# First modulation loads on two queues, with a new opening order: a two-layer decoder trunk on one Trainium2 core

## The chip, the cores and the metric

The kernel runs on one core of a Trainium2 chip. The metric is the device time of one execution in microseconds (us). Before the change the median of 3 runs is 1925.78 us (1925.18 to 1926.59). A core has a matrix engine (TensorE, PE in the profile; PEld is its weight load), a vector engine (VectorE, DVE), a scalar engine (ScalarE, ACT), GpSimd (POOL) and a sync engine (SP). Each works through its own list of instructions in order. A transfer is issued by one of them, here by SP or ACT, and is then moved by 16 DMA engines that all issuers share. Engines wait for each other, and for transfers, by semaphores.

## The reference

Two layers, 512 rows, 2048 columns, all in float32. Only the start matters here: the modulation of the first layer, and the first products of its input projection.

```python
c_act = jax.nn.silu(c)                                  # c: (1, 2048)
mod = c_act @ w_mod[l] + b_mod[l]                       # w_mod[l]: (2048, 6144)
shift, scale, gate = jnp.split(mod, 3, axis=-1)
h = x * (1.0 + scale[:, None]) + shift[:, None]         # x: (1, 512, 2048)
proj = h @ w_in                                         # w_in: (2048, 8192)
q, k, v, g = jnp.split(proj, 4, axis=-1)
```

Differential attention, an output projection and a layer norm follow, then a second layer with forgetting attention. The change touches none of that.

## The kernel before

**Products.** A float32 product is made of three fast ones: each operand is split into a rounded high part and the rest. `A` is high by high, `B` takes the rest of the input `h`, `C` the rest of the weights. A product is one matmul of 128x128 by 128x512.

**The opening** computes shift and scale of the first layer, builds `h` from them, and meanwhile runs the input projection of the first two heads (u = 0 and 1). The contraction of 2048 goes in 16 blocks of 128, `kt` = 0 to 15. Block `kt` of `h` needs columns `kt` of shift and of scale, and each of these columns is a sum over all 16 row blocks of `w_mod`. `SETS` orders these column blocks: first block 0 alone, then block 1 alone, then pairs. So the first set is 2 MB of `w_mod` (8 loads of 256 KB: two halves of 8 row blocks, each in two parts, each for shift and for scale), the second set another 2 MB, and every later set 4 MB.

The steps are single letters; each engine's order is a string of them (`ORDER_SP`, `ORDER_ACT`, `ORDER_PE`, `ORDER_DVE`, lines 41 to 44), written by a planner outside the kernel:

- SP: `L` is one load of `w_mod` into a tile `sms`, `X` a piece of `x` into `xt`, `W` a tile of projection weights `wst` (two transfers). W0 is the first tile for head 0's q and k (384 columns), W1 for its v and g, W2 and W3 the same for head 1.
- DVE: `d` adds one row block, times the matching value of `silu(c)`, to the running sum `sacc` (line 618; the first one of a set is line 616); `m` writes the finished columns of shift and scale to `mcol` (line 671); `b` makes the rest `wlo` of a weight tile (line 132), `l` the rest `hl` of a block of `h` (line 709).
- PE: `e` takes single row blocks of `w_mod` off DVE's hands (`PE_ROWS`: row blocks 6, 9, 10 and 13 of the first set, 9, 13 and 15 of the second); `o` sums `sacc` over its partitions; `t` transposes a block of `x`; `F` is a filler matmul with no result; `A`, `B`, `C` are the products (line 720).
- ACT: `a` casts a weight tile to its high part `whi` (line 125); `h` and `i` apply shift and scale to a transposed block of `x` (lines 694 and 701: `hh`, and `htmp` for the rest); `c` and `r` move partial sums out of PSUM and back.

So the first column goes: 12 `d` on DVE, `o` on PE, `m` on DVE, `h` on ACT, first product on PE. The same chain follows for block 1 and for each later set.

**Before the strings** a fixed prologue stands outside the opening's block: loads of `c` (`crow`) and of the biases (`brow`), their transposes, `silu(c)` into `cact`, the biases into `bcol`. All loads of the opening go through SP; eight loads of `w_mod` stand at the head of its string. A function `op_L` issues a load; it already takes a queue as an argument.

**Completion semaphores.** The framework hands eight completion semaphores (DMAHW0 to DMAHW7) to the transfers in turn. Each finished transfer adds 16. A transfer that takes a semaphore over waits, on the engine that issues it, until the transfer that had it before has landed.

Of the kernel before, what the change touches and what calls it, by code (L numbers as in the profile page):

```python
# [13 lines left out]
AF = mybir.ActivationFunctionType  # L14
ALU = mybir.AluOpType

P = 128
D = 2048
KT = D // P
# [18 lines left out]
PE_ROWS = {0: (6, 9, 10, 13), 1: (9, 13, 15)}  # L38
EARLY = (0,)
NBUF = 5  # L40
ORDER_SP = '8LX2LWLW7LX2LW2LW2LXW2LW4LWLWLXLWLWLW7LWLW3LWLX2L2WLW2LW3L2WLW2L2W2LW4LW2LWX4LW2L8Wp'
ORDER_ACT = 'ahiahia5ca2cahiahicracrcracrcrcrcrahiahia2c2rcrcrcrcracrahihi3ahiahicra2c2racrcrcracrhihai3ahihiacracrcrcrcracrcrhiahi3acracrcrcr3crc2r6c'
ORDER_PE = '4eFto7F3A3B3CABeCAB2eCABCABoCt7A7B7CABCABCABCABCABCABCABAB2CABCABCABCAoBCtABCABC2AtA3B3C6A6B5CACBCABCABCABCABCABCABCABCABCABCABCABCABCAoBCtABCABCABtCABCABCABCABCABCABCABCABCABCABCABCABCABCABCABCABCABCABCABCABoCABCABCABtCABCABCABtCABCABCABCABCABCABCABCABCABCABCABCABCABCABCABCAoBCtABCABC2AtA3B3C5A5B5CABCABCABCABCABCABCABCABCABCABCABCABCABCABCABCoABtCABCABCABtCABCABCABCABCABCABCABCABCABCABCABCABCABCABCABCABCABCABCABCABCABCABCAoBCABtCABCABCABtCABCABCABCABCABCABCABCABCABCABCABCABCABCABCABCABCABCABoCABtCABCABCABCABtCABCABCABCABCABCABCABCABCABCABCABCABCABCABCABCABCAB2AB2CBCABCABCABCABCABCABCABCABCABCABCABCABCABCABCABCABCABCABCABCABCABCABCABCABCABCABCABCABCABCABC'
ORDER_DVE = '13dm3dbldb9dm3dl3db5db4dmb2dldbl6db3db4dmb2dldbldb14dbmdb3dldl4db5dbmbdldbl6db3db5dbm5dbl3dbl6db2dbm4dl2dlb5db5dbmlbl4b'
MANUAL = {ET.DVE, ET.PE, ET.Activation, ET.SP}
CUT = False
LAM_INIT = 0.8 - 0.6 * math.exp(-0.0)
# [97 lines left out]
def tile_yoco(  # L145
# [23 lines left out]
    nc = tc.nc  # L169
    V, S, PE, G = nc.vector, nc.scalar, nc.tensor, nc.gpsimd  # L170
# [25 lines left out]
    def tr_bank(name="tr"):  # L196
        return ps.tile([P, 512], F32, name=name, tag="tr", bufs=1)
# [14 lines left out]
    def corner(sc, q, k):  # L212
# [6 lines left out]
    ident = const.tile([P, P], F32, name="ident")  # L219
# [3 lines left out]
    mask = const.tile([P, 512], F32, name="mask")  # L223
# [7 lines left out]
    crow, brow = (  # L231
        kpool.tile([P, T], F32, name=name, tag="K")[:k, 0:P]
        for name, k in (("crow", KT), ("brow", 32))
    )
    nc.sync.dma_start(crow, c[0].rearrange("(a p) -> a p", p=P))
    nc.sync.dma_start(brow, b_mod[0, 0 : 2 * D].rearrange("(a p) -> a p", p=P))
    ccol = const.tile([P, KT], F32, name="ccol")
    pcol = const.tile([P, 38], F32, name="pcol")
    bcol = const.tile([P, 2, KT], F32, name="bcol")
    pt = tr_bank()  # L240
    PE.transpose(pt[:, 0:KT], crow, ident[0:KT, 0:KT])
    V.tensor_copy(ccol, pt[:, 0:KT])
    cact = const.tile([P, KT], F32, name="cact")
    tc.keep_in_program_order(S.activation(cact, ccol, AF.Exp, scale=-1.0))
    V.tensor_scalar(cact, cact, 1.0, None, op0=ALU.add)
    V.reciprocal(cact, cact)
    V.tensor_tensor(cact, cact, ccol, op=ALU.mult)
    pt = tr_bank()
    PE.transpose(pt[:, 0:32], brow, ident[0:32, 0:32])
    V.tensor_copy(bcol[:, 0, :], pt[:, 0:16])  # L250
    V.tensor_scalar(bcol[:, 1, :], pt[:, 16:32], 1.0, None, op0=ALU.add)
    gcol, bncol = pcol[:, 0:16], pcol[:, 16:32]

    neglam = const.tile([P, 1], F32, name="neglam")
# [232 lines left out]
    with tc.tile_pool(name="start", bufs=2, reuse_waits="tile") as sp, tc.manual_schedule(engines=MANUAL):  # L487
        mcol = const.tile([P, 2, KT], F32, name="mcol")

        fill = kpool.tile([P, T], F32R, name="fill", tag="K")  # L490
        S.copy(fill[:, 0:384], mask[:, 0:384])
        tiles = []
        for i, (k0, nk) in enumerate(sets):
            nr = 8 // nk
# [41 lines left out]
        cnt = dict.fromkeys("LXWpdmlbahicretoABCF", 0)  # L536
# [22 lines left out]
        def op_L(j, queue=None):  # L559
            n, kq, step, v = loads[j]  # L560
            i, k, nr = tiles[n]
            k0, nk = sets[i]
            if n not in mtile:
                if n >= NBUF and not rows_read(n - NBUF):
                    return False
                mtile[n] = sp.tile([P, nr, 2, nk * P], F32, name="sms", tag="sms", bufs=NBUF)
            rows = w_mod[0, (k + kq) * P : (k + kq + step) * P, v * D + k0 * P : v * D + (k0 + nk) * P]
            (queue or nc.sync).dma_start(mtile[n][:, kq : kq + step, v, :], rows.rearrange("(k p) n -> p k n", p=P))  # L568
            return True
# [226 lines left out]
        kinds = ("LXWp", "ahicrK", "etoABCF", "dmlb")  # L796
        for text, kind in zip(lists, kinds):
            for ch in kind:
                if ch not in "KF":
                    text += [ch] * (total[ch] - text.count(ch) - (text.count("K") if ch == "L" else 0) - (lists[1].count("K") if ch == "L" else 0))  # L800
        at = [0] * 4
        while any(a < len(t) for a, t in zip(at, lists)):
            moved = False
# [1038 lines left out]
```

## Time and profile before

| What | Value |
|---|---|
| median of 3 runs | 1925.78 us |
| the profiled execution: its time, and its span | 1927.05 us, 1925.3 us |
| TensorE busy, share of the span | 1910.1 us, 99% |
| DVE, ACT busy | 1371.0 us (71%), 732.9 us (38%) |
| chain that ended last: PE, DVE, SP's queue, DMA | 96%, 2%, 1%, 1% |
| granted TensorE clock | 0.999 |

The span is the time from the first to the last instruction of the program in the profile; the time of a run also has what lies around it, 1.75 us in the profiled execution. Times in the views are microseconds from the start of the span. In a timeline a row gives start, duration, engine, line, operation, tiles, how many equal instructions it stands for, and in brackets how long the engine had been idle and what ended that. In the chain of waits a row gives start, duration and what it was.

### The profile page before, as it was taken

The page shows a single profiled execution, that of the slowest core. Times are in us where ns is not written, and L with a number is a line of the kernel's source. Part 1 is how long each engine was busy: PE and PEld are TensorE (multiplying, and loading weights), DVE is VectorE, ACT ScalarE, POOL GpSimd, SP SyncE. Part 2 cuts the span into 40 slices and gives each one's busy share as a digit, 9 for nine tenths or more (in the row PEclk, how much of TensorE's full clock was granted, in tenths as well). Part 3 has the DMA queues.
Part 4 walks back from the last instruction along what each step waited for, and adds up shares of the span by engine and source line. Part 5 has one row for each costly group of instructions (what it writes and reads, how often), then busy time and mean ns, then how long its engine had stood idle before and what let it go on. Part 6 is the DMA issues. An engine that isn't in the chain of part 4 may idle for free.

```text
span 1925.3 us, 25879 instructions
## 1 busy us (share of the span) xinstructions
PE 1910.1 (99%) x8921; PEld 1593.8 (83%) x8921; DVE 1371.0 (71%) x2617; ACT 732.9 (38%) x1266; POOL 2.3 (0%) x11
## 2 busy tenths in 40 slices
PE   8999999999999999999999999999999999999998
PEld 6888888888888888888888898888888888888887
DVE  7994588777776768667675477777566666686768
ACT  3656344333332344521272232224344344453122
POOL 0000000000000000000000000000000000000000
PEclk9999999999999999999999999999999999999999
DMA  9993566676767676476547586775345555555622
GB/s 339 385 339 91 158 187 197 209 239 189 235 197 225 203 225 182 123 241 221 184 164 251 181 297 209 250 266 162 112 147 159 158 150 162 154 153 168 226 93 110
DMA packets 352275, 382.22 MB, mean 199 GB/s; under 512 B 77912, under 2 KB 256244, under 8 KB 351376
## 3 DMA queue, kind: packets, MB, share of 16 engines
q1 hardware_dynamic: 349120, 376.25, 61.7%
q10 hardware_dynamic: 3024, 4.33, 0.6%
q8 instruction: 70, 1.15, 0.2%
q14 instruction: 61, 0.50, 0.1%
HBM read 348.68 MB, written 31.80 MB: 198 GB/s over the span
## 4 chain that ended last, share of the span: by engine, by line
PE 96%; DVE 2%; SPq 1%; DMA 1%; issue 0%; ACT 0%; DVEq 0%; ACTq 0%
PE acc L208 26%; PE acc L209 26%; PE acc L210 26%; PE acc L720 4%; PE sc L720 2%; PE sc L210 1%; PE sc L209 1%; PE sc L208 1%; PE o L208 1%; PE o L210 1%; PE o L209 1%; PE o L720 1%; SPq L568 1%; DMA sms<-in_w_mod_dram 0%; PE tr L686 0%
## 5 line engine op out<-in xcount | busy, mean ns | idle before, releaser
L113 ACT CAST whi<-wst 128x1024 fp32r<-128x1024 f32 (+2 forms) x298 | 303.4, 1018 | 616.4 <-PE acc L210 314.1
L114 DVE TENSOR_TENSOR wlo<-wst,whi 128x1024 fp32r<-128x1024 f32 (+2 forms) x298 | 351.4, 1180 | 248.5 <-ACT whi L113 222.7
L208 PE MATMUL acc<-hh,whi 128*128 128x512 f32 x1184 | 463.2, 391 | 0.0
L209 PE MATMUL acc<-hl,whi 128*128 128x512 f32 x1184 | 462.0, 390 | 0.0
L210 PE MATMUL acc<-hh,wlo 128*128 128x512 f32 x1184 | 460.3, 390 | 0.0
L208 PE MATMUL acc<-whi,hh 128*128 128x512 f32 (+1 forms) x1104 | 418.8, 380 | 0.0
L209 PE MATMUL acc<-wlo,hh 128*128 128x512 f32 (+1 forms) x1104 | 417.0, 378 | 0.0
L210 PE MATMUL acc<-whi,hl 128*128 128x512 f32 (+1 forms) x1104 | 416.5, 378 | 0.0
L433 DVE SCALAR_TENSOR_TENSOR macc<-ms,cact,macc 128x512 f32<-128x512 f32 x307 | 228.9, 746 | 61.2 <-DMA ms<-in_w_mod_dram 44.4
L210 PEld LDWEIGHTS acc<-hh,wlo 128*128 128x128 f32 x1184 | 222.4, 188 | 47.0
L208 PEld LDWEIGHTS acc<-hh,whi 128*128 128x128 f32 x1184 | 222.5, 188 | 44.1 <-DVE sgb L1509 0.8
L209 PEld LDWEIGHTS acc<-hl,whi 128*128 128x128 f32 x1184 | 222.6, 188 | 42.2
L210 PEld LDWEIGHTS acc<-whi,hl 128*128 128x128 f32 x1104 | 207.4, 188 | 38.6
L208 PEld LDWEIGHTS acc<-whi,hh 128*128 128x128 f32 x1104 | 207.4, 188 | 37.5 <-DVE ztmp L1241 0.6
L209 PEld LDWEIGHTS acc<-wlo,hh 128*128 128x128 f32 x1104 | 207.5, 188 | 35.6
L618 DVE SCALAR_TENSOR_TENSOR sacc<-sms,cact,sacc 128x512 f32<-128x512 f32 (+1 forms) x128 | 89.9, 702 | 6.2 <-DMA sms<-in_w_mod_dram 2.9
L904 ACT ACTIVATE e<-e,mn 128x128 f32<-128x128 f32 (+3 forms) x64 | 36.0, 563 | 111.1 <-DVE mn L900 104.5
L1559 ACT ACTIVATE eb<-eb,mnb 128x128 f32<-128x128 f32 (+1 forms) x64 | 35.9, 561 | 73.8 <-DVE mnb L1556 73.5
L720 PE MATMUL acc<-wlo,hh 128*128 128x512 f32 x128 | 49.9, 399 | 0.6 <-DVE wlo L132 0.6
L720 PE MATMUL acc<-whi,hl 128*128 128x512 f32 x128 | 49.4, 394 | 0.0
L720 PE MATMUL acc<-whi,hh 128*128 128x512 f32 x128 | 49.2, 393 | 0.0
L132 DVE TENSOR_TENSOR wlo<-wst,whi 128x768 fp32r<-128x768 f32 (+1 forms) x32 | 34.8, 1088 | 17.3 <-ACT whi L125 16.2
(336 smaller groups left out, 2095.6 us busy)
## 6 DMA issues: line engine op xcount, KB each, us to landing
wst<-in_a_w_in_dram SPq DMA_DIRECT2D x240, 256.0 KB
ms<-in_w_mod_dram SPq DMA_DIRECT2D x136, 256.0 KB
ms<-in_kv_w_mod_dram SPq DMA_DIRECT2D x64, 512.0 KB
wst<-in_b_w_in_dram SPq DMA_DIRECT2D x128, 256.0 KB
sms<-in_w_mod_dram SPq DMA_DIRECT2D x56, 512.0 KB
wst<-in_kv_w_dram SPq DMA_DIRECT2D x56, 512.0 KB
ms<-in_w_mod_dram SPq DMA_DIRECT2D x32, 512.0 KB
wst<-in_a_w_out_dram SPq DMA_DIRECT2D x32, 512.0 KB
```

The costliest lines, as they stand in the source:

```text
L113: self.nc.scalar.copy(hi[:, :, :w], st[:, :, :w])
L114: self.nc.vector.tensor_tensor(lo[:, :, :w], st[:, :, :w], hi[:, :, :w].bitcast(F32), op=ALU.subtract)
L132: self.nc.vector.tensor_tensor(lo[:, :, :w], st[:, :, :w], hi[:, :, :w].bitcast(F32), op=ALU.subtract)
L208: PE.matmul(dst, lhs[0], rhs[0], start=start, stop=False, skip_group_check=True)
L209: PE.matmul(dst, lhs[0], rhs[1], start=False, stop=False, skip_group_check=True)
L210: PE.matmul(dst, lhs[1], rhs[0], start=False, stop=stop, skip_group_check=True)
L433: ins = V.scalar_tensor_tensor(acc, w, cact[:, kt : kt + 1], acc, op0=ALU.mult, op1=ALU.add)
L568: (queue or nc.sync).dma_start(mtile[n][:, kq : kq + step, v, :], rows.rearrange("(k p) n -> p k n", p=P))
L618: V.scalar_tensor_tensor(acc, w, sc, acc, op0=ALU.mult, op1=ALU.add)
L720: PE.matmul(bank[n, bk], l, r, start=start, stop=stop, skip_group_check=True)
L904: S.activation(e[:, :w], e[:, :w], AF.Exp, bias=mn, scale=-1.0, accum_out=rs)
L1559: S.activation(e[:, :w], e[:, :w], AF.Exp, bias=mn, scale=-1.0, accum_out=rs)
```

## The change

1. The prologue moves from the top of the kernel into the block whose order is written by hand, and is mixed with the eight loads of the first set. These are no longer all SP's: ACT issues the first, third, sixth and eighth, SP the other four. ACT's first two stand ahead of its table load and `silu`, its last two behind the cast `fill`.
2. All four strings are new: the loads of SP, and above all the order of PE's products, which before went mostly in `ABC` triples and now mixes products of several banks.
3. Three of the eight fillers `F` go. Nothing else is added or removed; behind the opening every engine's order is the same as before.

```diff
-ORDER_SP = '8LX2LWLW7LX2LW2LW2LXW2LW4L...'
+ORDER_SP = '2LX6LW4LXW7LW3LW2LWLXL2W3L...'
-ORDER_PE = '4eFto7F3A3B3CABeCAB2eCABCABoCt7A7B7CABCABC...'
+ORDER_PE = '4eFotFA2FAFBA2B3ABeBCBe2Ceo2CtCABAC5A2B2CA2BABCABC...'
...
-    nc.sync.dma_start(crow, c[0].rearrange("(a p) -> a p", p=P))
-    nc.sync.dma_start(brow, b_mod[0, 0 : 2 * D].rearrange("(a p) -> a p", p=P))
...
+        def first_loads(*queues):
+            for queue in queues:
+                op_L(cnt["L"], queue)
+                cnt["L"] += 1
+                del lists[0][lists[0].index("L")]
+
+        nc.sync.dma_start(crow, c[0].rearrange("(a p) -> a p", p=P))
+        nc.sync.dma_start(brow, b_mod[0, 0 : 2 * D].rearrange("(a p) -> a p", p=P))
+        first_loads(nc.scalar, nc.sync, nc.scalar, nc.sync)
+        pt = tr_bank()
+        PE.transpose(pt[:, 0:KT], crow, ident[0:KT, 0:KT])
...
+        S.copy(fill[:, 0:384], mask[:, 0:384])
+        first_loads(nc.sync, nc.scalar, nc.sync, nc.scalar)
```

`first_loads` takes eight `L` off SP's new string, so behind the shared loads SP goes on with `XW4LXW7LW...`.

The first place is ACT at the very start, with the semaphores that each instruction waits for. Before:

```order
L244 ACT_TABLE_LOAD
L244 ACTIVATE cact<-ccol 128x16 [waits DVE_49]
L491 CAST fill<-mask 128x384 [waits Pool_49]
L125 CAST whi<-wst 128x2x384 [waits DMAHW6_49,DMAHW5_49]
L694 ACTIVATE hh<-px,mcol 128x512 [waits DVE_49]
L701 ACTIVATE htmp<-px,mcol 128x512
```

Now:

```order
L554 DMA sms<-in_w_mod_dram 128x4x128 x2
L799 ACT_TABLE_LOAD
L799 ACTIVATE cact<-ccol 128x16 [waits DVE_49]
L807 CAST fill<-mask 128x384 [waits Pool_49]
L554 DMA sms<-in_w_mod_dram 128x4x128 [waits DMAHW0_49]
L554 DMA sms<-in_w_mod_dram 128x4x128 [waits DMAHW2_49]
L125 CAST whi<-wst 128x2x384 [waits DMAHW1_49]
L680 ACTIVATE hh<-px,mcol 128x512 [waits DVE_49,PE_49]
```

ACT's third and fourth load wait for a completion semaphore each. The second place is SP over the same stretch, now:

```order
L793 DMA crow<-in_c_dram 16x128
L794 DMA brow<-in_b_mod_dram 32x128
L554 DMA sms<-in_w_mod_dram 128x4x128 x4
L564 DMA xt<-in_x_dram 128x4x128 [waits DMAHW0_49]
L63 DMA wst<-in_a_w_in_dram 128x2x256 [waits DMAHW1_49]
L63 DMA wst<-in_a_w_in_dram 128x2x128 [waits DMAHW2_49]
L554 DMA sms<-in_w_mod_dram 128x4x128 [waits DMAHW3_49]
```

Before, SP had all eight loads of the first set ahead of `xt`, and two more between `xt` and the first `wst`; now `xt` and `wst` follow on four. DMAHW0 is handed first to ACT's first load, then to `xt`, then to ACT's third load; DMAHW2 to `brow`, then to the second transfer of `wst` (128 columns), then to ACT's fourth load. In the built program ACT's third load waits for DMAHW0 at 32, its fourth for DMAHW2 at 32.

The third place is DVE from the first set on. Before:

```order
L616 TENSOR_SCALAR sacc<-sms,cact 128x2x128
L618 SCALAR_TENSOR_TENSOR sacc<-sms,cact,sacc 128x2x128 x11
L616 TENSOR_SCALAR sacc<-sms,cact 128x2x128
L671 TENSOR_TENSOR mcol<-tr,bcol 128x2
L618 SCALAR_TENSOR_TENSOR sacc<-sms,cact,sacc 128x2x128 x3
L132 TENSOR_TENSOR wlo<-wst,whi 128x2x384
L709 TENSOR_TENSOR hl<-htmp,hh 128x512
L618 SCALAR_TENSOR_TENSOR sacc<-sms,cact,sacc 128x2x128
L132 TENSOR_TENSOR wlo<-wst,whi 128x1024
L618 SCALAR_TENSOR_TENSOR sacc<-sms,cact,sacc 128x2x128 x8
```

Now:

```order
L602 TENSOR_SCALAR sacc<-sms,cact 128x2x128
L604 SCALAR_TENSOR_TENSOR sacc<-sms,cact,sacc 128x2x128 x11
L132 TENSOR_TENSOR wlo<-wst,whi 128x2x384
L602 TENSOR_SCALAR sacc<-sms,cact 128x2x128
L657 TENSOR_TENSOR mcol<-tr,bcol 128x2
L604 SCALAR_TENSOR_TENSOR sacc<-sms,cact,sacc 128x2x128 x4
L695 TENSOR_TENSOR hl<-htmp,hh 128x512
L604 SCALAR_TENSOR_TENSOR sacc<-sms,cact,sacc 128x2x128 x3
L132 TENSOR_TENSOR wlo<-wst,whi 128x1024
L604 SCALAR_TENSOR_TENSOR sacc<-sms,cact,sacc 128x2x128 x5
```

The rest of the first weight tile (`wlo`) now stands ahead of the first column (`mcol`), where before it stood behind it; the number of sums between the first and the second column is 12 in both.

More of the change, by code (lines that the diff above doesn't have):

```diff
@@ L40 @@
 NBUF = 5
[L41 to L44, printed above, removed]
+ORDER_SP = '2LX6LW4LXW7LW3LW2LWLXL2W3LW3LX2LW2LWLW3LW2LW3LW3LXLWLWLWLW3L2W2LW2LW2LW3LWLXLW4L4W2L3Wp3W'
+ORDER_ACT = 'ahiahia6cacahiahicrcac2r2cracrc2rhiahiacar2crc2rcracrcrahihi2ahihiacrcarcar2crcrarcrahi2ahiahiahia2crc2racrcrcrcr2ahaihaia2crca2r2c2r2c2r7c'
+ORDER_PE = '4eFotFA2FAFBA2B3ABeBCBe2Ceo2CtCABAC5A2B2CA2BABCABCBAB2CBA2B2CAB2C4AB2A2B2ABAB2C2BCBoBCt5CA2CAtA2B2CBC6ABCA3BCBAB3CABC2B2A2C2BC2ACBCBA2CBACABCA2BABC2ABoCAt3AB2CBCBAtACABABCA2CBCBA2B2CBCABCBACBABCABACACBCBCACB2ABAC2B2A2CBCABABACoBA2CACBAtCABCABABtA2BACBAB3CA2CA2BCAC2B3A2BACA2CBC2BACABA2BABoB2CtCACB2C2At2C2B4AB3CBAC2A3BC2B2CACABCABAB2CB3ACBCBABAB2CACBA2C2B2ABCAB3CABCA2BC2A2B4Ao2ABCAtACBAC2BC2ACB2ABCBC2B2CBA3C2BAtABCA2BAB2ACBABC2AC2B2A2CBA2CoBAtABACBC2BCBCBCtCABCACBCABCBACBAC2A2CBA2CBACABCB2ACBABAB2AB5CBA2B3AC2B2C3B2ACA4CBA2B2ACAC2ACA2B2A2BCA2C2BABAo2Bt3CB2ABCB3ABABCB2C2BAB3CA2Ct3C3ABACABACBCBCABC2B2ACBA2CBCBA2BC2AC3BC2A2CBCB2AC2A2B2A2C2BC2B2ACAC2BAB4CACBCABCBC'
+ORDER_DVE = '12dbdm4dl3db5dm3dl5db8dbmb2dl2dlb4db8dbm2dl2dbl4d2b8dbm3db5dldl7dbmdlbl2db3db5dbdb7dm2db6dlbdl4dbmdlb3dl2dbd2b8dbdm2b2l3b'
 MANUAL = {ET.DVE, ET.PE, ET.Activation, ET.SP}
@@ L239, in tile_yoco @@
     bcol = const.tile([P, 2, KT], F32, name="bcol")
-    pt = tr_bank()
-    PE.transpose(pt[:, 0:KT], crow, ident[0:KT, 0:KT])
-    V.tensor_copy(ccol, pt[:, 0:KT])
     cact = const.tile([P, KT], F32, name="cact")
[L244 to L251, printed above, removed]
     gcol, bncol = pcol[:, 0:16], pcol[:, 16:32]
@@ L490, in tile_yoco @@
         fill = kpool.tile([P, T], F32R, name="fill", tag="K")
-        S.copy(fill[:, 0:384], mask[:, 0:384])
         tiles = []
@@ L800, in tile_yoco @@
                     text += [ch] * (total[ch] - text.count(ch) - (text.count("K") if ch == "L" else 0) - (lists[1].count("K") if ch == "L" else 0))
+        def first_loads(*queues):
[8 more added lines that the diff above has]
+        PE.transpose(pt[:, 0:KT], crow, ident[0:KT, 0:KT])
+        V.tensor_copy(ccol, pt[:, 0:KT])
+        S.activation(cact, ccol, AF.Exp, scale=-1.0)
+        V.tensor_scalar(cact, cact, 1.0, None, op0=ALU.add)
+        V.reciprocal(cact, cact)
+        V.tensor_tensor(cact, cact, ccol, op=ALU.mult)
+        pt = tr_bank()
+        PE.transpose(pt[:, 0:32], brow, ident[0:32, 0:32])
+        V.tensor_copy(bcol[:, 0, :], pt[:, 0:16])
+        V.tensor_scalar(bcol[:, 1, :], pt[:, 16:32], 1.0, None, op0=ALU.add)
+        S.copy(fill[:, 0:384], mask[:, 0:384])
+        first_loads(nc.sync, nc.scalar, nc.sync, nc.scalar)
         at = [0] * 4
```

## The prediction

> **What bounds the kernel now.** I read the shares of the page and the chain that ended last first, then the windows of the first 260 us, then the timelines of DVE, PE and ACT over the first 40 us, and last the transfers.
>
> ```profile
> PE 1910.1 (99%) x8921; PEld 1593.8 (83%) x8921; DVE 1371.0 (71%) x2617; ACT 732.9 (38%) x1266; POOL 2.3 (0%) x11
> PE 96%; DVE 2%; SPq 1%; DMA 1%; issue 0%; ACT 0%; DVEq 0%; ACTq 0%
> 0.00:10.00 10.00, 3.32 (x13) 2.82 (x13) 4.59 (x14) 1.90 (x3) 1.60 (x9) 1.00 0.71 205
> 10.00:20.00 10.00, 9.57 (x43) 8.50 (x44) 8.10 (x17) 3.17 (x4) 0.00 (x0) 1.00 1.13 355
> 20.00:30.00 10.00, 9.13 (x47) 7.27 (x47) 9.47 (x17) 3.17 (x5) 0.00 (x0) 1.00 1.09 380
> 30.00:40.00 10.00, 9.34 (x44) 7.22 (x44) 7.56 (x10) 4.52 (x8) 0.00 (x0) 1.00 1.09 381
> 40.00:50.00 10.00, 10.00 (x50) 8.29 (x50) 9.35 (x14) 5.63 (x9) 0.00 (x0) 1.00 1.09 383
> ```
>
> In a window row the first busy number is PE's. From 40 us on PE is never idle: whatever the opening does later, its end is set by when PE gets its work and by how much work that is. All that a new order can win or lose lies ahead of 40 us. The work itself does not change: 672 products, which cost the same in a run on one bank (5.44 / 24 = 0.227 us) as in turns between banks (0.45 / 2), so PE's new mixed order is free:
>
> ```profile
> 68.05 5.44 PE acc L720 x24
> 99.50 0.45 PE sc L720 x2
> 100.18 0.45 PE acc L720 x2
> ```
>
> Ahead of 40 us PE waits for the two first columns, that is for DVE, and DVE for the loads:
>
> ```profile
> 11.10 1.52 DVE L618 SCALAR_TENSOR_TENSOR sacc<-sms,cact,sacc 128x256 f32<-128x256 f32 x3 [0.48 <-DMA sms<-in_w_mod_dram]
> 13.89 0.16 DVE L671 TENSOR_TENSOR mcol<-tr,bcol 128x2 f32<-128x2 f32 x1 [0.17 <-PE tr L660]
> 16.62 0.69 DVE L709 TENSOR_TENSOR hl<-htmp,hh 128x512 fp32r<-128x512 f32 x1 [0.26 <-ACT htmp L701]
> 18.83 4.12 DVE L618 SCALAR_TENSOR_TENSOR sacc<-sms,cact,sacc 128x256 f32<-128x256 f32 x8
> 14.41 0.83 ACT L125 CAST whi<-wst 128x768 fp32r<-128x768 f32 x1 [10.71 <-DMA wst<-in_a_w_in_dram]
> 15.14 0.77 ACT L694 ACTIVATE hh<-px,mcol 128x512 fp32r<-128x512 f32 x1
> 15.97 0.73 PE L720 MATMUL sc<-hh,whi 128*128 128x512 f32 x2
> 25.39 0.73 PE L720 MATMUL sc<-hh,whi 128*128 128x512 f32 x2 [0.87 <-ACT hh L694]
> ```
>
> The first set has landed just ahead of 11.10, the sums end at 12.62, the first column stands at 14.05, the first product runs at 15.97. The second set's sums end at 18.83 + 4.12 = 22.95, and block 1's first product is 2.44 us behind that, at 25.39. Between these products PE has only block 0's 21 products to do (21 x 0.227 = 4.8 us), so 25.39 is what counts. Behind it PE loses time twice more before it is saturated:
>
> ```profile
> 35.04 0.39 PE L720 MATMUL acc<-whi,hl 128*128 128x512 f32 x1
> 36.03 0.74 PE L720 MATMUL acc<-wlo,hh 128*128 128x512 f32 x2 [0.60 <-DVE wlo L132]
> 39.14 1.02 PE tr L660 x8
> 58.25 0.79 PE tr L660 x8
> ```
>
> 0.99 - 0.23 = 0.76 us waiting for W3's rest, and 1.02 - 0.79 = 0.23 us in the next `o`.
>
> **The change part by part.** *The shared issue.* SP issues `crow`, `brow` and then the eight loads:
>
> ```profile
> 0.73 0.40 SPq L235 DMA_DIRECT2D crow<-in_c_dram  x1
> 1.19 0.41 SPq L236 DMA_DIRECT2D brow<-in_b_mod_dram  x1
> 1.64 5.58 SPq L568 DMA_DIRECT2D sms<-in_w_mod_dram  x8
> 2.10 0.51 SPq L568
> 6.44 0.78 SPq L568
> GB/s 0 7 51 251 292 193 283 328 326 322 345 339 366 350 376 366 346 346 347 368 385 382 360 383 387 382 369 386 387 377 372 387 385 383 385 373 373 383 385 386
> ```
>
> ACT can issue at 0.73 what SP issued at 1.64, so the stream of bytes starts 0.91 us earlier. That is the gain, and little more: an issue takes 0.51 us, while the stream moves 256 KB in 0.73 us. (From the first set's landing at 11.1 to W0's at 14.4 came `xt`, two loads and W0, 1.18 MB in 3.3 us.) From 3 us on the bytes limit, not the issuer.
>
> The Trainium skill, "DMA: Bandwidth & Descriptors", section "Issuing engines are not separate DMA queues", says as much: several issuers save only the issuing time, since all transfers interleave on the same 16 engines. By that rule the sharing can win no more than these 0.91 us.
>
> *The two late loads.* ACT's third and fourth loads, pieces 6 and 8 of the first set, wait until DMAHW0 and DMAHW2 stand at 32, which means until `xt` and until W0 have landed. Before, no piece of this set waited for either. `xt` is now the seventh transfer of 256 KB; before, the seventh landed one load ahead of the eighth, 11.05 - 0.73 = 10.3; 0.91 earlier is 9.4. W0 has 384 KB more, 1.1 us: 10.5. So piece 6 is issued at 9.4 and piece 8 at 10.5. From issue to landing the trace has three prices: 3.2 us on an empty queue (second load, issued 2.10, used at 5.30), 4.6 us on a full one (eighth load, issued 6.44, used at 11.10), and 8.45 us, the longest of this stretch:
>
> ```profile
> 5.30 0.35 DVE L616 TENSOR_SCALAR sacc<-sms,cact 128x256 f32<-128x256 f32 x1 [1.01 <-DMA sms<-in_w_mod_dram]
> 23.16 8.45 DMA sms<-in_w_mod_dram
> ```
>
> At 10.5 SP's queue is full, so I take 4.6: piece 8 lands at 15.1, 4.0 us later than before. Three sums need it (row blocks 12, 14, 15), so the first set's sums end at 15.1 + 1.52 = 16.6.
>
> The same page's "Queues, rings and completion order" has each DMA engine take turns between queues. By it piece 8 would not stand behind SP's backlog but get half the rate: 3.2 + 0.73 = 3.9 us, landing 14.4, and the sum below would be 0.7 us smaller. No run here shows a loaded SP queue beside ACT's in the opening, so both stay inside the bounds.
>
> *The first column.* Now `wlo` and a sum stand ahead of `mcol`:
>
> ```profile
> 28.89 0.95 DVE L132 TENSOR_TENSOR wlo<-wst,whi 128x768 fp32r<-128x768 f32 x1
> 29.75 0.74 DVE L618 SCALAR_TENSOR_TENSOR sacc<-sms,cact,sacc 128x512 f32<-128x512 f32 x1
> 13.37 0.35 DVE L616 TENSOR_SCALAR sacc<-sms,cact 128x256 f32<-128x256 f32 x1 [0.74 <-DMA sms<-in_w_mod_dram]
> 17.69 1.22 DVE L132 TENSOR_TENSOR wlo<-wst,whi 128x1024 fp32r<-128x1024 f32 x1
> ```
>
> 0.86 (start to start) + 0.4 + 0.16 brings it to 18.05, against 14.05; PE's `o` is done beside that. `hh` follows at 18.1 (15.14 before, where it stood behind the cast of W0) and the first product 0.83 later at 18.9. That is 2.9 us late, but alone it would cost nothing, since block 1 is waited for anyway.
>
> *The second column.* Behind `mcol` DVE has twelve sums (4.12 / 8 = 0.515 each, 6.2 us), `hl` (0.69) and W1's rest (1.22): 8.1 us, ending at 26.15. Before it also had W0's rest there. Its loads are SP's and keep to the earlier stream. Plus 2.44, block 1's first product runs at 28.6 instead of 25.39: **+3.2 us**. Twenty products instead of 21 are done by then: +0.2.
>
> *What comes back.* W3 has 9.7 MB ahead of and with it in either order of SP, so its cast is no later, while PE wants it 3 us later: the 0.76 and the 0.23 go, **-1.0 us**. The three fillers go into idle time, nothing. Behind 40 us every window of before is full and the steps keep their numbers: nothing.
>
> Sum: 3.2 + 0.2 - 1.0 = **+2.4 us**; I take 2.2, since a little of PE's slack in other small gaps will be eaten too. The profiled execution took 1927.05 us (span 1925.3 and 1.75 around it), 1.27 above the median of the runs; it would become 1929.2, the median **1928.0 us**. Bounds: with 3.2 us for piece 8 the sum is 1.4 smaller, +0.8; with 8.45 it is 3.85 larger, +6.0.
>
> **The rivals.** *The last pieces land far later* (slower). ACT's loads come into a queue that SP keeps full, and piece 8 behind piece 6; the 8.45 us row is the price that the trace has for a deep queue, so piece 8 lands at 19, and DVE, which takes its steps in order, can do nothing of the second set meanwhile. +6.0 us: 1931.8. It decides as soon as piece 8 lands behind 16.6, where the loss passes 0.2%. For it: 1.13 in the share column of 10 to 20 us, transfers without a gap. Against: that row is from 23 us, when loads were twice as large.
>
> *The late loads are hidden.* If pieces 6 and 8 land by 12, because `xt` and W0 land early and the price is the empty queue's, DVE's 12 sums end near 13 and what is left is the earlier stream and the stalls: 25.39 becomes about 25.4, less 1.0: 1924.8. Against: piece 8 cannot be issued before W0 has landed, and W0 needs 2.2 MB moved, which at these rates is 9.5 at the earliest.
>
> *The plan works as if there were no wait* (faster). All of the first set lands 0.9 earlier, DVE ends at 11.7, `mcol` at 13.1, block 1's first product at 13.1 + 8.1 + 2.44 = 23.65, 1.7 early, less 1.0: -2.7 us, 1923.1. Even that is within 0.2%; more would need stalls that PE does not have. So the change can hardly be measured as faster.
>
> **How the numbers follow.** About 0.2%, 3.85 us, is what a measurement of this kernel tells from no change. The forecast, +0.8 to +3.8: 0.48. Late landing beyond that: 0.32. Hidden: 0.13. The plan without the wait: 0.07, of which 0.04 past 0.2%, by something I do not see. So faster 0.04, same 0.64, slower 0.32. The range runs from 1924.6, just under the hidden case, to 1932.2, just over the late one; the forecast's own is 1926.6 to 1929.6.
>
> **What would show it.** In the profile after: ACT issues two loads near 9.4 and 10.5 us; DVE idles, ended by a load of `sms`, until about 15, and its first set ends near 16.6 instead of 12.62; `mcol` near 18; first products at 18.9 and 28.6; no wait for `wlo` at 36 us; PE full behind 41. Wrong if the first set's sums end by 13.5 (hidden), or not before 19 (late), or if PE shows new idle time behind 45 us, which no term here allows for.

## The result and the profile after

The changed kernel takes 1932.23 us (median of 7 runs, 1930.85 to 1933.29), the kernel before 1926.22 us beside it (median of 7, 1925.18 to 1927.72). The ratio is 1.0029, 95% interval 1.0019 to 1.0039: **slower by 6.0 us, 0.3%**. Measured once more (run e8 below) the ratio is 1.0030, 1.0019 to 1.0042. The profiled execution of the changed kernel has a span of 1930.4 us, 5.1 more than that of before. That is less than 6.0 since before's profiled execution, 1927.05 us, lay 0.8 above its median and the change's, 1932.23, on it.

The busy times of the page look like before's:

```profile
PE 1910.1 (99%) x8918; PEld 1592.7 (83%) x8918; DVE 1370.1 (71%) x2617; ACT 730.6 (38%) x1266; POOL 2.3 (0%) x11
```

PE is busy exactly as long as before, 1910.1 us. The time was lost as idle time of PE, and the windows of the first 50 us say where (first busy number: PE):

```profile
0.00:10.00 10.00, 2.86 (x10) 2.37 (x10) 4.13 (x13) 1.90 (x3) 1.60 (x9) 1.00 0.84 251
10.00:20.00 10.00, 4.59 (x20) 4.18 (x20) 4.21 (x11) 0.83 (x1) 0.00 (x0) 1.00 1.09 335
20.00:30.00 10.00, 9.45 (x46) 7.82 (x45) 7.94 (x16) 2.41 (x4) 0.00 (x0) 1.00 1.09 383
30.00:40.00 10.00, 9.83 (x43) 7.60 (x42) 9.34 (x14) 7.63 (x12) 0.00 (x0) 1.00 1.09 380
40.00:50.00 10.00, 10.00 (x54) 8.34 (x53) 8.87 (x13) 3.84 (x5) 0.00 (x0) 1.00 0.92 304
```

From 10 to 20 us PE was busy for 9.57 us before and is for 4.59 now: 5.0 us gone there, and 0.5 in the first window. Between 20 and 40 us it regains 0.8 (9.45 + 9.83 against 9.13 + 9.34), and from 40 us on it is full but for waits of under a microsecond. The longest of them is one that before doesn't have; in e8 it is 0.90 us:

```profile
1024.51 0.50 PE L208 MATMUL acc<-whi,hh 128*128 128x512 f32 x1 [0.87 <-ACT hh L1341]
```

What starves PE stands in the timelines of ACT (its two late issues) and DVE:

```profile
9.46 1.50 ACTq L554 DMA_DIRECT2D sms<-in_w_mod_dram  x2
10.54 0.41 ACTq L554 DMA_DIRECT2D sms<-in_w_mod_dram  x1
...
14.94 1.00 DVE L604 SCALAR_TENSOR_TENSOR sacc<-sms,cact,sacc 128x256 f32<-128x256 f32 x2 [4.86 <-DMA sms<-in_w_mod_dram]
16.73 1.52 DVE L604 SCALAR_TENSOR_TENSOR sacc<-sms,cact,sacc 128x256 f32<-128x256 f32 x3 [0.79 <-DMA sms<-in_w_mod_dram]
...
19.36 0.16 DVE L657 TENSOR_TENSOR mcol<-tr,bcol 128x2 f32<-128x2 f32 x1
24.98 2.56 DVE L604 SCALAR_TENSOR_TENSOR sacc<-sms,cact,sacc 128x256 f32<-128x256 f32 x5
28.96 0.16 DVE L657 TENSOR_TENSOR mcol<-tr,bcol 128x2 f32<-128x2 f32 x1 [1.42 <-PE tr L646]
```

(The second row is the second of the two issues in the first, from a narrower window.) Pieces 6 and 8 are issued at 9.46 and 10.54 and used at 14.94 and 16.73: 5.5 and 6.2 us from issue to use. That the semaphores held them back shows in the trace: `xt` landed (the sixteenth increment of its semaphore) at 9.44, W0's second transfer at 10.52, each about 0.02 us ahead of an issue of ACT's. DVE idles for 4.86 us. The first set's sums end at 18.25, the first column starts at 19.36, the second set's sums end at 27.54, and then DVE waits another 1.42 us for PE's `o`. PE over the same stretch:

```profile
14.90 2.38 PE L632 MATMUL tr<-cact,sms 128*128 128x1 f32 x10 [6.32 <-DMA sms<-in_w_mod_dram]
21.14 0.80 PE L706 MATMUL sc<-hh,whi 128*128 128x512 f32 x1 [0.55 <-ACT hh L680]
23.12 0.63 PE L706 MATMUL sc<-hl,whi 128*128 128x512 f32 x1
23.55 0.63 PE L706 MATMUL o<-hh,whi 128*128 128x512 f32 x1
23.98 0.63 PE L706 MATMUL sc<-hl,whi 128*128 128x512 f32 x1
...
30.80 0.50 PE L706 MATMUL sc<-hh,whi 128*128 128x512 f32 x1 [0.17 <-ACT hh L680]
```

PE stood still for 6.32 us. Its first product comes at 21.14 (15.97 before), and block 1's first product at 30.80 (25.39 before): +5.4 us. And there is something the prediction had not: the products at 23.12, 23.55 and 23.98 start 0.43 us apart, not 0.227. They are the same matmuls of 128x128 by 128x512, nothing stands between them, and they wait for nothing. Two windows of the same trace show it too, with the granted clock (the third number from the right) at 1.00 in both:

```profile
21.00:24.40 3.40, 3.25 (x8) 2.64 (x9) 3.01 (x6) 1.69 (x3) 0.00 (x0) 1.00 1.09 382
24.80:28.00 3.20, 3.20 (x21) 2.80 (x20) 2.60 (x6) 0.00 (x0) 0.00 (x0) 1.00 1.09 384
```

8 matmuls in 3.25 us of busy time, then 21 (some of them small) in 3.20.

So there were two candidates for the loss: the late pieces, and a slow PE. A third was the new order by itself.

### The profile page after: what moved, and what is told of

It is laid out like the page before. It is cut to its first block, busy times and chain, and to the rows that moved or that the text cites. A ratio compares the mean times of both kernels' runs of the same rounds, so it can differ in the third digit from the quotient of the medians.

```text
span 1930.4 us, 25857 instructions
## 1 busy us (share of the span) xinstructions
PE 1910.1 (99%) x8918; PEld 1592.7 (83%) x8918; DVE 1370.1 (71%) x2617; ACT 730.6 (38%) x1266; POOL 2.3 (0%) x11
## 3 DMA queue, kind: packets, MB, share of 16 engines
q8 instruction: 70, 1.15, 0.2%
## 4 chain that ended last, share of the span: by engine, by line
PE 97%; DVE 1%; DMA 1%; SPq 0%; ACT 0%; issue 0%; DVEq 0%; ACTq 0%
PE acc L208 27%; PE acc L209 26%; PE acc L210 26%; PE acc L706 5%; PE sc L706 2%; PE sc L210 1%; PE sc L209 1%; PE sc L208 1%; PE o L208 1%; PE o L706 1%; PE o L210 1%; PE o L209 1%; DMA sms<-in_w_mod_dram 0%; PE tr L646 0%; PE tr L672 0%; DMA n<-turned_n 0%
## 5 line engine op out<-in xcount | busy, mean ns | idle before, releaser
L706 PE MATMUL acc<-whi,hh 128*128 128x512 f32 x128 | 45.1, 393 | 0.0
L706 PE MATMUL acc<-wlo,hh 128*128 128x512 f32 x128 | 44.8, 396 | 0.0
L909 DVE CUSTOM_DVE_ANT_0 e<-sc,bias 128x256 f32<-128x256 f32 (+2 forms) x48 | 26.5, 551 | 24.7 <-PE sc L210 24.6
```

Source lines behind the costliest of these rows:

```text
L706: PE.matmul(bank[n, bk], l, r, start=start, stop=stop, skip_group_check=True)
L909: V.tensor_tensor_reduce(out=e[:, :w], in0=sc[:, :w], in1=bias, scale=-1.0, scalar=3.0e38, op0=ALU.add, op1=ALU.min, accum_out=mn,)
```

## The experiments

All times are medians; "before" is the kernel before on the same chip and in the same rounds. A profiled execution can lie some 3 us from its kernel's median (e3's span of 1933.0 with 1.75 us around it is 2.8 above, e9's 1.4 below), so what a run says of the mechanism is read from its rows, and of the time from its median. The ratio isn't the quotient of the two medians (1.0031 for the change), so the last two columns can differ by some tenths of a microsecond.

| Run | Orders | First set's loads | Fillers ahead of the first product | Ratio to before, 95% interval | us to before |
|---|---|---|---|---|---|
| the change | new | 4 on ACT, 2 of them late | 2 | 1.0029 (1.0019 to 1.0039) | +6.0 |
| e8, the change again | new | the same | 2 | 1.0030 (1.0019 to 1.0042) | +5.5 |
| e3 | old | 4 on ACT, 2 late | 8 | 1.0028 (1.0017 to 1.0039) | +5.3 |
| e7 | new | 2 late ones on SP | 2 | 1.0022 (1.0012 to 1.0031) | +3.9 |
| e11 | new | only piece 6 late | 2 | 1.0018 (1.0009 to 1.0027) | +3.9 |
| e4 | new | 4 on ACT, 2 late | 46 | 1.0017 (1.0008 to 1.0026) | +3.1 |
| e1 | new | all on SP, none late | 2 | 1.0004 (0.9995 to 1.0013) | +1.2 |
| e9 | new | all on SP, none late | 14 | 1.0003 (0.9994 to 1.0012) | +1.0 |
| e5 | new | 2 on ACT, none late | 14 | 0.9999 (0.9990 to 1.0008) | -0.3 |
| e2 | new | 2 on ACT, none late | 2 | 0.9996 (0.9987 to 1.0005) | -0.6 |
| e10 | old | 2 on ACT, none late | 15 | 0.9998 (0.9989 to 1.0007) | 0.0 |
| e6, e12 | old | 2 on ACT, none late | 8 | 0.9995 (0.9987 to 1.0004), 0.9991 (0.9982 to 1.0000) | -0.8, -1.3 |

### Who is to blame: the late pieces, the order, or the second queue

**e1: all eight loads back on SP, new orders kept.**

```diff
-        first_loads(nc.scalar, nc.sync, nc.scalar, nc.sync)
+        first_loads(nc.sync, nc.sync, nc.sync, nc.sync)
...
-        first_loads(nc.sync, nc.scalar, nc.sync, nc.scalar)
+        first_loads(nc.sync, nc.sync, nc.sync, nc.sync)
```

> The changed kernel with its new orders, but all eight loads of the first set issued by SP, one behind the other as before; ACT issues none, so no load waits for xt or W0. My theory (the two late loads carry the whole loss): the first set's sums end near 12.6 us again, the first column near 15 (W0's rest now stands ahead of it), block 1's first product near 25.5, and the time is 1926.2 us, within 1 us of before and 6 us under the changed kernel. Rival A (the new orders cost the time by themselves, above all PE's mixed products): the sums end at 12.6 just the same, but products from 45 us on are still about 5 us later than before and the time stays near 1931.

Measured: 1927.87 us against 1926.65. Most of the loss is gone, and the interval (0.9995 to 1.0013) holds no change, but rows of DVE and PE are not where I had them:

```profile
11.63 1.52 DVE L604 SCALAR_TENSOR_TENSOR sacc<-sms,cact,sacc 128x256 f32<-128x256 f32 x3 [0.85 <-DMA sms<-in_w_mod_dram]
14.29 0.96 DVE L132 TENSOR_TENSOR wlo<-wst,whi 128x768 fp32r<-128x768 f32 x1 [1.14 <-ACT whi L125]
25.48 0.16 DVE L657 TENSOR_TENSOR mcol<-tr,bcol 128x2 f32<-128x2 f32 x1 [2.15 <-PE tr L646]
...
18.92 0.63 PE L706 MATMUL o<-hh,whi 128*128 128x512 f32 x1
19.34 0.63 PE L706 MATMUL sc<-hl,whi 128*128 128x512 f32 x1
27.33 0.50 PE L706 MATMUL sc<-hh,whi 128*128 128x512 f32 x1 [0.16 <-ACT hh L680]
```

The sums end at 13.15, and the column is held up for 1.14 us because W0's rest now stands ahead of it. Then PE runs at half rate again (18.92, 19.34), DVE waits 2.15 us for its `o`, and block 1's first product comes at 27.33, not 25.5. So rival A is not right, but it isn't nothing either: by the rows the new orders have a cost of their own in the opening, which the time doesn't tell from none.

**e2: ACT issues only pieces 1 and 3, which wait for nothing.** The second call of `first_loads` is `(nc.sync, nc.sync, nc.sync, nc.sync)`, the first as in the change.

> The changed kernel, but ACT issues only the first two of its loads (pieces 1 and 3), which wait for nothing; the other six go to SP. My theory: the 0.9 us of earlier issue are won and nothing is lost, the first set's sums end near 11.7 us, block 1's first product runs near 24.6, and the time is 1925.3 us, 0.9 under before. Rival B (a load on a second queue beside SP's is slow in itself, 5.4 to 6.1 us from issue to landing as in the changed kernel): pieces 1 and 3 land near 6.3 and 7.2 us instead of 4.5 to 5.3, the first set's sums end no sooner than before (12.6 us), and the time is 1926.2 or more.

Measured: 1926.01 against 1926.65, -0.6, not told from no change. The sums end at 12.31, between the two theories. Block 1's first product is 1.5 us sooner than in e1, but again after a wait for PE:

```profile
6.23 0.35 DVE L602 TENSOR_SCALAR sacc<-sms,cact 128x256 f32<-128x256 f32 x1 [1.52 <-DMA sms<-in_w_mod_dram]
6.62 5.69 DVE L604 SCALAR_TENSOR_TENSOR sacc<-sms,cact,sacc 128x256 f32<-128x256 f32 x11
23.95 0.16 DVE L657 TENSOR_TENSOR mcol<-tr,bcol 128x2 f32<-128x2 f32 x1 [1.86 <-PE tr L646]
...
17.61 0.63 PE L706 MATMUL o<-hh,whi 128*128 128x512 f32 x1
18.04 0.63 PE L706 MATMUL sc<-hl,whi 128*128 128x512 f32 x1
25.80 0.50 PE L706 MATMUL sc<-hh,whi 128*128 128x512 f32 x1 [0.17 <-ACT hh L680]
```

DVE starts later than before (6.23 against 5.30: the first sum needs a load of either queue) but then does all eleven sums without a gap. DVE itself, not the loads, now sets the end of the set. By the semaphores ACT's pieces 1 and 3 landed at 3.80 and 4.95 us, so the slow second queue of rival B isn't there. It was SP's first one, piece 2, that came late, at 6.10 (the second load of before: 5.17). The last piece landed at 10.02, 0.96 us sooner than before's at 10.98: the earlier issue did bring the loads forward.

The products start 0.43 us apart here too (17.61, 18.04), although PE idled for no longer than 1.13 us at a time from 8 us on. The half rate doesn't need a long wait for a late piece.

**e3: the old order strings, loads shared as in the change.**

```diff
-ORDER_SP = '2LX6LW4LXW7LW...'
+ORDER_SP = '8LX2LWLW7LX2LW...'
```

and the other three strings likewise.

> The order strings of before with the loads shared as in the changed kernel: ACT's third and fourth load wait again for transfers that SP issues behind them (xt, and the second set's second load). My theory: the loss comes from the sharing alone, the first set's sums end between 16.5 and 18.5 us, block 1's first product runs 4.5 to 6 us late, and the time is 1931.3 us. Rival A (the new orders are what costs): 1926.2 us, as before, or up to 0.9 less.

Measured: 1931.99 against 1926.65, +5.3; expected 1931.3. The sharing alone brings a loss of the same size under the old orders. Rows of DVE:

```profile
16.49 1.01 DVE L604 SCALAR_TENSOR_TENSOR sacc<-sms,cact,sacc 128x256 f32<-128x256 f32 x2 [6.49 <-DMA sms<-in_w_mod_dram]
18.54 1.52 DVE L604 SCALAR_TENSOR_TENSOR sacc<-sms,cact,sacc 128x256 f32<-128x256 f32 x3 [1.05 <-DMA sms<-in_w_mod_dram]
```

In this execution, the slowest of e3's seven (1934.79), the pieces come later still, and the sums end at 20.06, outside the 16.5 to 18.5 that I had expected.

**e7: the two late pieces on SP's queue,** at the place in time where ACT had issued them. `first_loads` leaves out pieces 6 and 8, and a new letter `Y` issues them in SP's string:

```diff
-ORDER_SP = '2LX6LW4LXW7LW...'
+ORDER_SP = '2LX6LW4LYXYW7LW...'
...
-        first_loads(nc.sync, nc.scalar, nc.sync, nc.scalar)
+        first_loads(nc.sync, None, nc.sync, None)
...
+        def op_Y(j):
+            return op_L((5, 7)[j])
```

> The changed kernel, but pieces 6 and 8 are issued by SP, not by ACT, at about the place in time at which ACT issued them: behind the second set's four loads (near 9.6 us) and behind the second xt (near 10.9 us). Nothing waits for xt or W0 to land, and there is one queue only. Theory 1 (the price of 5.4 and 6.1 us from issue to landing comes from the second queue beside SP's full one): on SP's own queue it is 4.7 us, piece 8 lands near 15.6, the first set's sums end near 17.1 instead of 18.25, block 1's first product is about 1.1 us earlier, 1931.1 us. Rival D (the price is that of the backlog, on whichever queue): piece 8 lands near 17 us, sums end at 18.3 or later, 1932.2 us. Either way about 4 to 6 us slower than before, since what counts is how late the two pieces are issued; if the time came out near before's, my theory of the late pieces would fall.

Measured: 1930.57 against 1926.65, +3.9. Late pieces cost without a second queue and without a wait for `xt` or W0. Rows of SP (its issue of piece 8) and of DVE:

```profile
11.64 0.69 SPq L554 DMA_DIRECT2D sms<-in_w_mod_dram  x1
...
16.12 1.53 DVE L607 SCALAR_TENSOR_TENSOR sacc<-sms,cact,sacc 128x256 f32<-128x256 f32 x3 [0.52 <-DMA sms<-in_w_mod_dram]
```

Piece 8 took 4.5 us from issue to use here, near the 4.7 of theory 1, and 5.9 to 6.2 on ACT (10.54 to 16.73 in the change; 10.26 to 16.13 in e8). But SP got to it only at 11.64, 0.7 later than planned, so it was there no earlier than e8's, between the 15.6 of theory 1 and the 17 of rival D. The trace of the change speaks for rival D. There SP's own transfers issued at 8.77, 9.65 and 10.47 us landed, by their semaphores, at 14.27, 15.31 and 16.74, after 5.5, 5.7 and 6.3 us; ACT's, issued at 9.46 and 10.54, at 14.86 and 16.65. So the higher price isn't one of ACT's queue: beside each other both engines' transfers pay it, and they land nearly in the order of issue.

**e11: only piece 6 late.** Piece 8 goes back to SP: the second call is `first_loads(nc.sync, nc.scalar, nc.sync, nc.sync)`.

> The changed kernel with piece 8 given back to SP; only piece 6 still waits on ACT until the transfer that now bears the same semaphore has landed, which by this order is the seventh piece or the eighth one and no longer xt. My theory: piece 6 is issued about 0.7 us earlier than in the changed kernel, near 8.6 us, and lands near 13.5; the sums of row blocks 12 to 15 follow it without another wait and end near 16 instead of 18.25 us; PE is still at half rate, so block 1's first product comes near 29 us, and the time is about 3.5 us over before: 1930.2. Rival F (the loss is the last piece's alone, piece 6 is covered by other sums): 1927 to 1928, as with all loads on SP.

Measured: 1930.98 against 1927.12, +3.9 (3.5 expected); rival F falls. ACT, DVE and PE:

```profile
9.16 0.46 ACTq L554 DMA_DIRECT2D sms<-in_w_mod_dram  x1
...
14.04 2.57 DVE L604 SCALAR_TENSOR_TENSOR sacc<-sms,cact,sacc 128x256 f32<-128x256 f32 x5 [4.61 <-DMA sms<-in_w_mod_dram]
...
30.25 0.51 PE L706 MATMUL sc<-hh,whi 128*128 128x512 f32 x1 [0.16 <-ACT hh L680]
```

One late piece holds DVE for 4.61 us; the sums behind it run through. It was issued at 9.16, not at 8.6: what it waited for, piece 8 by its semaphore, landed at 9.14, about as late as `xt` had. From issue to use it took 4.9 us.

### What the slow PE costs

**e4: the change, with PE kept busy** while it has nothing to do, by 44 more fillers; **e8: the change again,** to stand beside it.

```diff
-ORDER_PE = '4eFotFA2FAFBA...'
+ORDER_PE = 'e28F2e6Fe5Fot7FA2FAFBA...'
```

> The changed kernel with 43 more filler products on PE, placed where PE idles between 8 and 21 us, so that it is busy when the first products come; nothing else differs. My theory (PE ran its products 0.43 us apart there because it had idled for 6.3 us, and that made the second set's o and with it block 1 about 0.7 us later): the products behind 21 us run 0.227 us apart, the wait of DVE for the second set's o falls from 1.42 to about 0.7 us, block 1's first product is 0.7 us earlier, and the time 1931.5 us. Rival C (the 0.43 us is set by something else, such as the loads or the weights that PE reads): products still 0.43 us apart, block 1 unchanged, 1932.2 us. The time alone can hardly tell these apart; the rows of the products do.

> The changed kernel itself, once more beside the others: 1932.2 us, 5.6 over before, products behind 21 us 0.43 us apart, the wait for the second set's o near 1.4 us. It is here to be compared with the run that kept PE busy (3.1 us over before): if it comes out 5 to 6 us over before again, the fillers were worth 2 to 3 us and not the 0.7 that I gave them; if nearer 4, the gain was mostly scatter between launches.

Measured: e4 1929.71 (+3.1), e8 1932.17 (+5.5). By the medians the fillers were worth 2.4 us, more than the 0.7 that I gave them. The medians are from two chips and their intervals overlap (to 1.0026 and from 1.0019), but in the two profiles the last piece is used at the same moment, which makes them a clean pair. DVE and PE of e8:

```profile
16.13 1.52 DVE L604 SCALAR_TENSOR_TENSOR sacc<-sms,cact,sacc 128x256 f32<-128x256 f32 x3 [0.96 <-DMA sms<-in_w_mod_dram]
29.30 0.16 DVE L657 TENSOR_TENSOR mcol<-tr,bcol 128x2 f32<-128x2 f32 x1 [2.35 <-PE tr L646]
...
31.15 0.50 PE L706 MATMUL sc<-hh,whi 128*128 128x512 f32 x1 [0.17 <-ACT hh L680]
```

And of e4:

```profile
16.13 1.52 DVE L604 SCALAR_TENSOR_TENSOR sacc<-sms,cact,sacc 128x256 f32<-128x256 f32 x3 [1.33 <-DMA sms<-in_w_mod_dram]
27.21 0.16 DVE L657 TENSOR_TENSOR mcol<-tr,bcol 128x2 f32<-128x2 f32 x1 [0.70 <-PE tr L646]
...
21.86 0.40 PE L706 MATMUL o<-hh,whi 128*128 128x512 f32 x1
22.09 0.39 PE L706 MATMUL sc<-hl,whi 128*128 128x512 f32 x1
29.05 0.50 PE L706 MATMUL sc<-hh,whi 128*128 128x512 f32 x1 [0.17 <-ACT hh L680]
```

With the same loads, block 1's first product comes at 29.05 with a PE kept busy and at 31.15 without: 2.1 us, of which 1.65 is the shorter wait for `o` (0.70 against 2.35). The products are 0.23 us apart, not 0.43. Rival C falls: the half rate comes from how little PE had done before, not from the loads or the weights. This is shown; that it costs 2.1 us in every execution is not (in the first profile of the change that wait was 1.42).

**e5: fillers with two loads on ACT; e9: fillers with all loads on SP.** In both the string of PE begins `e5F3e4Fot5FA...`.

> The run with two loads on ACT (no load waits for another), and 14 fillers on PE instead of 2 ahead of the first product, so that PE is busy from 5 us on. My theory (two separate costs: the wait of the late loads, now gone, and a PE that runs its first products at half rate because it idled before): the products behind 15 us run 0.227 us apart, DVE's wait for the second set's o falls from 1.86 to under 0.8 us, block 1's first product comes near 24.6 us instead of 25.80, and the time is 1 us under the run with two loads alone and about 1.5 us under before: 1925.1 where before is 1926.65. Rival C (the half rate has another cause than PE's idling): products still 0.43 us apart, block 1 at 25.8, 1926.0.

> All eight loads on SP, the new orders, and 14 fillers on PE ahead of the first product instead of 2: the run with all loads on SP (1927.87, 1.2 over before) with PE kept busy. My theory (the 1.2 us over before is PE at half rate, whose wait for the second set's o was 2.15 us there): products 0.227 us apart from 18 us on, that wait near 0.7 us, block 1's first product near 25.8 us instead of 27.33, and a time 0 to 1.5 us under that run: about 1926.8, level with before. Rival A' (what costs is that the new DVE order puts W0's rest ahead of the first column, 1.1 us of waiting there): the column still stands 1.5 us later than before and the time stays near 1927.9.

Measured: e5 1926.35 (e2 had 1926.01), e9 1928.12 against a before of 1927.12 (+1.0; e1 had +1.2). The medians show no gain from fillers where no piece is late. In e5's rows the wait for `o` did fall to 0.70, but in this execution, the slowest of e5's eleven (1929.26), PE then met the next bound:

```profile
23.47 0.16 DVE L657 TENSOR_TENSOR mcol<-tr,bcol 128x2 f32<-128x2 f32 x1 [0.70 <-PE tr L646]
29.95 3.12 DVE L604 SCALAR_TENSOR_TENSOR sacc<-sms,cact,sacc 128x512 f32<-128x512 f32 x4 [2.63 <-DMA sms<-in_w_mod_dram]
...
25.31 0.50 PE L706 MATMUL sc<-hh,whi 128*128 128x512 f32 x1 [0.16 <-ACT hh L680]
33.98 0.50 PE L706 MATMUL sc<-hh,wlo 128*128 128x512 f32 x1 [1.44 <-DVE wlo L132]
```

Block 1 was there at 25.31, half a microsecond sooner than in e2, and then DVE waited for loads of the third set until 29.95, and PE, behind it, until 33.98. That every execution gives its lead back in this way isn't shown. By the time, rival A' is nearer for e9. Its rows of DVE and PE leave room for both:

```profile
14.71 0.16 DVE L657 TENSOR_TENSOR mcol<-tr,bcol 128x2 f32<-128x2 f32 x1
24.08 0.16 DVE L657 TENSOR_TENSOR mcol<-tr,bcol 128x2 f32<-128x2 f32 x1 [1.19 <-PE tr L646]
...
25.93 0.50 PE L706 MATMUL sc<-hh,whi 128*128 128x512 f32 x1 [0.17 <-ACT hh L680]
```

The column is 0.8 us later than before's 13.89, the wait for `o` is down from 2.15 to 1.19, and block 1 comes 1.4 us sooner than in e1. This is the fastest of e9's eleven executions (1926.75); that the gain doesn't appear in the median stays unexplained.

### Two loads shared, in the old orders

**e6 and e12: the orders of before, pieces 1 and 3 on ACT.** Old strings, the moved prologue, `first_loads(nc.scalar, nc.sync, nc.scalar, nc.sync)` and then four on SP.

> The order strings of before, with only pieces 1 and 3 on ACT and the other six on SP, so no load waits for another. My theory: the same steps as before, all up to block 1 about 0.9 us sooner (sums end near 11.7, block 1's first product near 24.5 us), PE's products 0.227 us apart since the old order has seven fillers ahead of them; 0.9 us under before: 1925.7. Rival B (a second queue beside SP's slows the set's loads): sums end at 12.3 to 12.6 as before, 1926.65 or more.

> The orders of before with pieces 1 and 3 on ACT, once more: the run with the lowest median so far, 0.8 us under before with an interval that still holds no change. If the earlier issue is worth its 0.9 us, it comes out 0.5 to 1 us under before again; if the first result was scatter, level with before.

Measured: 1925.86 (-0.8) and 1925.73 (-1.3); the second interval ends at 1.0000. Against the change it is 6 to 7 us less. Against before it is a gain of about 1 us at the edge of what can be measured. In e6 the first column starts at 13.24 and block 1's first product at 24.62 (13.89 and 25.39 before); rows of DVE and PE:

```profile
13.24 0.16 DVE L657 TENSOR_TENSOR mcol<-tr,bcol 128x2 f32<-128x2 f32 x1 [0.77 <-PE tr L646]
...
24.62 0.74 PE L706 MATMUL sc<-hh,whi 128*128 128x512 f32 x2 [0.87 <-ACT hh L680]
```

**e10: the same with seven more fillers,** PE's string beginning `e4F3e4Fto7F3A...` in place of `4eFto7F3A...`.

> The orders of before with two loads on ACT (1925.86, the lowest median so far), and eight more fillers on PE ahead of the first o, so that it is at full rate when o is due. My theory: o takes 0.6 us instead of 1.01, the first column stands 0.3 us earlier (12.9), block 1's first product near 24.3 us; 0.3 us under that run, 1925.5, which no measurement tells from it. Rival E (more fillers delay the transposes or the o themselves): the first column later than 13.24, and 1926.2 or more.

Measured: 1927.14 against 1927.12; rival E came out. A row of DVE:

```profile
14.43 0.16 DVE L657 TENSOR_TENSOR mcol<-tr,bcol 128x2 f32<-128x2 f32 x1 [1.76 <-PE tr L646]
```

The column stands 1.2 us later than in e6: the fillers themselves ran at half rate and stood in the way of `o`.

## Why the prediction came out as it did

The sign and the place were right, and so was the first half of the mechanism, the two late loads; its second half, a slow PE, was missing. The likeliest case was too small: 1928.0, and 1932.2 came out. No change beyond 0.2% had a chance of 0.64, a loss beyond it 0.32; the loss came. The time stands at the very end of the range (1932.23 against 1932.2; as a difference from before, +6.0 against +6.4). That it isn't clearly beyond is in part luck: this end was worked out from 8.45 us for piece 8, which no late load took; a smaller delay and a slow PE came to the same sum. By its steps:

- **The late issue** at 9.4 and 10.5 us: 9.46 and 10.54.
- **The price of the late loads**, taken as 4.6 us from the full queue's row: this is the first term that was mis-sized. It measured 5.5 and 6.2 us in the change, 4.9 to 6.2 in e4, e8 and e11. The last piece was used at 16.73, not 15.1: +1.6 us. The row that I took was from a kernel in which SP alone issues. In e7, where SP issues the late pieces, piece 8 took 4.5; with both engines issuing, SP's own transfers took 5.5 to 6.3 as well. The upper bound of 8.45 was not reached.
- **The turns between queues**: the Trainium skill, "DMA: Bandwidth & Descriptors", section "Queues, rings and completion order", says that each DMA engine takes turns between the queues that it has work for. The estimate that I worked out from it was 3.9 us for piece 8. The runs show 5.9 to 6.2, and no gain over SP's own transfers beside it; the measurement decides against the estimate. Why the turns don't help here is open.
- **The way from the last piece to block 1**, 13.5 us in the prediction (28.6 - 15.1): 14.07 in the change, 15.02 in e8, 12.92 in e4 (from the last piece's use to the product). So with a full-rate PE I had reckoned 0.6 too much, having added up durations of DVE where steps overlap; the half rate then cost 1.15 and 2.1 us on top, which no term of mine held. **This is the step that failed**: "Twenty products instead of 21 are done by then: +0.2" and "The three fillers go into idle time, nothing" both took a product at 0.227 us whatever PE had done before; it was 0.43. I called idle time free, and it isn't only the 6.32 us: in e2, with no idle time above 1.13 us from 8 us on, the products are as slow. One part came out by luck: the 2.44 us from the second set's last sum to the product were read in an order in which the third set's first sum (at 23.01, 0.49 us) stands ahead of the second column; in the new one it stands behind, and e4 has 2.54 all the same.
- **Block 1's first product**: +3.2 forecast, +5.4 measured (30.80 against 25.39); of the 2.2 between them 1.6 come from the loads, 0.6 from this way.
- **What comes back**, -1.0: by the start times of the products in the two traces the gap is 5.4 us at block 1's first product and 4.5 at the 84th, -0.9. No wait for W3's rest at 36 us is left.
- **Nothing behind 40 us**: in the change PE waits behind 45 us for no more than 0.22 us at a time until 1020 us, as forecast. But the sign of being wrong that I had named, new idle time behind 45 us, did come: at 1024 us PE waits 0.87 us for ACT's `hh` (0.90 in e8), and the gap between the traces, 4.1 us ahead of it, is 5.1 by the end (4.9 and 6.0 in e8). e5, e11 and e2 have this wait too (1.11, 0.30 and 0.32 us); in before and the other runs, e1, e4 and e7 among them, it isn't there. So it doesn't go with the late pieces; whether the change brings it or the single execution is not shown.
- **The mixed product order is free**: nothing measured speaks against it behind 25 us. But the new orders cost in the opening what I had not booked to them: W0's rest ahead of the first column (1.14 us of waiting in e1), and too few matmuls ahead of the first product to bring PE to its rate (block 1 at 24.62 in e6, at 25.80 in e2; their times, -0.8 and -0.6, don't tell them apart).
- **The rivals**: the number that came out is that of "the last pieces land far later", +6.0 us, and its point of decision, piece 8 behind 16.6 us, was passed by a tenth. In e8, with the same loss, it wasn't: piece 8 was used at 16.13. Its mechanism came out by half: the piece was 2.3 us earlier than that case had it, and a slow PE did the rest. "Hidden" and "as if there were no wait" fell; e2, in which no load waits for another, comes nearest to the latter: -0.6 us, less than the -2.7 reckoned.
- **No more than 0.9 us to be won by sharing**: e6 and e12, -0.8 and -1.3, agree within their intervals.

## What to carry to other kernels

Before a load is put on a second queue, look which transfer had its completion semaphore before: a load that shares one with a later, bigger transfer waits for it, and the engine that issues it waits too. Price a late load by what all issuing engines together have in flight ahead of it, not by a row of one queue, and follow it until the last thing that hangs on it. Idle time on PE, even in gaps of a microsecond, is only free if what follows doesn't need PE at its full rate within the next few microseconds; fillers help there, but only where they aren't ahead of something that is waited for.

## What the runs showed of the hardware that was not expected

- **A matmul's rate depends on what PE did before, and the granted clock in the profile doesn't show it.** After 6 us of idling, products of 128x512 start 0.43 us apart in the change, later 0.227, with the granted clock at 1.00 in both windows; in e2 they do so after idle times of at most 1.13 us from 8 us on. In the change, e1, e2, e8 and e11 the rate doubled after 3.3 to 6.2 us of work without a gap (e1: from the first product at 16.51 to about 22.7). The Trainium skill, "TensorE: Matmul & The Clock Gate", section "What's actually happening", says that PE runs at half clock by default and after an idle window of about 3.4 us, and at full clock after a busy one, and that the window runs freely, so that the point varies from run to run; its section "Wait — 56ns, not 53.3ns?" gives 426.7 ns for this size at half clock. The traces agree with the 426.7 ns; the time until the rate doubled, 3.3 to 6.2 us, reaches beyond the 3.4.
- **A load on the less used queue isn't the quicker one; the loads of both queues wait alike.** Beside a full SP queue, ACT's late loads took 4.9 us from issue to use in the best case (e11, 9.16 to 14.04) and 7.5 in the worst: e3's second one was issued at 11.02 and used at 18.54. SP's own beside them took 5.5 to 6.3 in the change, from issue to landing. With SP alone issuing the late ones, e7's piece 8 took 4.5.
- **The whole stream of loads can fall behind by microseconds.** In e5 DVE waited 2.63 us for a load of the third set, in an execution in which nothing had been made later by the kernel. By the semaphores, e5's loads on SP land at most 0.94 us behind e2's, which are the same in the same order, up to 23.7 us; those that land at 25.87 and 29.82 are 1.5 and 3.0 us behind, though SP issued both only 0.7 us later, and the ones behind them stay late. Two executions of the same program lie closer: of the loads issued in the first 70 us none lands more than 1.15 us apart in the change and e8, or more than 0.45 us in e6 and e12. What held e5's stream is not shown.
